# First tiles fed k-outer behind the norm, and forgetting attention as one stream of steps across head borders, in a hybrid transformer layer

## The chip, the cores and the metric

The kernel runs on the 8 cores of one Trainium2 chip. Each core computes one of the eight sequences of the batch, with the same program; the cores exchange nothing. The metric is the device time in microseconds (us) of the slowest core. A trace also gives the span of each core, and where a difference of a few us is at stake this document uses the mean of the eight spans as well, because "the slowest of eight" adds luck to every reading.

Executions of this program come in two states. In the slow one the cores of one die show a lower granted TensorE clock than those of the other, and the time is some per cent longer.

## The reference

One layer: adaLN-modulated RMSNorm, one combined projection, eight heads of forgetting attention (FoX), eight heads of sliding-window attention with rotary embedding and sinks (SWA), output projection, and a squared-ReLU MLP. Sequence and model width are both 2048, head width is 128.

```python
h = rmsnorm(x, g_pre_mix) * (1.0 + sc_a) + sh_a        # sh, sc, gt = parts of silu(c) @ w_mod + b_mod
fq, fk, fv, fg, sq, sk, sv = split(h @ w_in)
log_f = log_sigmoid(fg + b_forget)
fox = forgetting_attention(fq, fk, fv, log_f)          # s[t,u] += cum[t] - cum[u], causal softmax
swa = sliding_window_sink_attention(rope(sq), rope(sk), sv, swa_sinks)
x = x + gt_a * rmsnorm(concat(fox, swa) @ w_out, g_post_mix)
h = rmsnorm(x, g_pre_mlp) * (1.0 + sc_m) + sh_m
x = x + gt_m * rmsnorm(square(relu(h @ w_up)) @ w_down, g_post_mlp)
```

## The kernel before

The program is written as a list of operations in program order; a helper records every operation (`pe` for matmuls, `act` for ScalarE, `cp`, `ts`, `tt`, `stt` for VectorE or GpSimd) and works out the semaphores. So all matmuls of the profile carry one line number, L387, all ScalarE operations L404, VectorE's L407 (two tensors), L412 (scalar and two tensors), L418 and L421 (copy); groups are told apart by the tiles in them.

The names that matter: a *bank* is one of the eight parts of PSUM, the memory into which TensorE writes its products and from which another engine has to read them before the bank is free again. `hT` is the normed input, transposed, in four tiles of 512 tokens and 16 chunks `k`. `R1` is a ring of five 0.5 MB buffers (`ring_67` to `ring_71` in the trace) for the projection's weight stripes, `qh` holds the first two q stripes, `RH` four buffers for the weights of the shift vector (`rsh`), `RM` those of the scale vector. `xstA` and `xstB` hold the input of even and odd tiles. The shift is not added to `hT`: each stripe instead gets a bias column, a product of the stripe with the shift vector `shb`.

The first tile is multiplied *k-outer* (the loop over the chunks is the outer one: each chunk is used by all products in turn, where k-inner finishes one product first) while its chunks are made; tiles 1 to 3 follow with one product after the other:

```python
    def wave0(k):
        h = hT(0, k)
        for i, b in enumerate((qh[0], R1.bufs[W["k"]])):
            pe([mm(banks[PJ[i]](), b(slice(k * 128, k * 128 + 128)), h, k == 0, k == KC - 1)], [b(), h], [banks[PJ[i]]()])
        b = R1.bufs[W["v"][k // 8]]
        kk = k % 8
        for i in range(2):
            ob = banks[OB[i]]
            pe([mm(ob(bi * 256, bi * 256 + 256), hT(0, k, slice((2 * i + bi) * 128, (2 * i + bi) * 128 + 128)),
                   b(slice(kk * 256, kk * 256 + 256)), k == 0 and bi == 0, k == KC - 1 and bi == 1) for bi in range(2)], [b(), h], [ob()])
        fg_mm(0, k, banks[SB[0]])
    # ... weight loads, statistics and norm of tile 0 and of tile 1 around wave0(0..15), cut ...
    F.side = [mods(0, F.pend)]
    for t in range(1, NT):
        jobs = {}
        if t + 1 < NT:
            def at(i, f):
                jobs.setdefault(i, []).append(f)
            for q in range(4):
                at(5 + 3 * q, lambda q=q: n_sq(t + 1, q))
                at(8 + 3 * q, lambda q=q: n_stat(t + 1, q))
            at(18, lambda: n_rstd(t + 1))
            for k in range(KC):
                at(19, lambda k=k: n_z(t + 1, k))
        last = t == NT - 1
        gens = [g_qh(0, t, ev_q(0)(t)), g_fm(sk0, t, ev_k(0)(t), last), g_fg(t)]
        gens += [g_v(sv0, 2 * t + i, vX, last and i == 1) for i in range(2)]
        i = 0
        for g in gens:
            for _ in g:
                for j in jobs.get(i, []):
                    j()
                i += 1
                if last and i % 4 == 0:
                    F._side()
        if t == 1:
            dma("pool", qh[1](), src1(("A", I_Q + 1)), "qh1")
            R1.start(3)
            x_load(3)
```

`g_qh`, `g_fm`, `g_fg` and `g_v` are generators that issue a quarter of a 16-chunk product (four 128x512 matmuls or their equal) and then yield; they take turns on two PSUM banks. The same generators are the *filler* of attention: `F.fill(w)` issues that much projection work between two steps of attention.

The bias columns of the rotary stripes, and a FoX step. A step (`h`, `j`, `kb`) has a score matmul (`qk`), a VectorE subtraction of the decay row and a ScalarE exponential (`expo`), and two products (`pv`). The decay row of head and tile is broadcast from DRAM into one of two buffers `cfb`:

```python
    def sw_bias(i, b):
        bk = fm_col(b, banks[SF[St.sb % 3]])
        act(bs(slice(i, i + 1)), bk(0, 1), AF.Copy)
        act(bsw(slice(i, i + 1), p=(0, 64)), bk(0, 1, p=(64, 128)), AF.Copy)
        act(bsw(slice(i, i + 1), p=(64, 128)), bk(0, 1, p=(0, 64)), AF.Copy)

    def cf_load(h, j):
        i = St.cf % 2
        St.cf += 1
        cf_slot[(h, j)] = cfb[i]
        dma("sp", cfb[i](), dram(T["crow"][h:h + 1, j * TS:j * TS + TS].broadcast_to([128, TS]), "crow", j), f"cf{i}")

    def fox_list(h):
        return [(h, j, kb) for j in range(NT) for kb in range(4 * j + 4)]

    def qk(st):
        h, j, kb = st
        if kb == 0:
            if (h, j) not in cf_slot:
                cf_load(h, j)
            nj = (h, j + 1) if j + 1 < NT else (h + 1, 0)
            if nj[0] < 8 and not (nj[1] == 0):
                cf_load(*nj)
        bk = banks[SF[St.sb % 3]]
        St.sb += 1
        c0 = max(0, kb - 4 * j) * 128
        diag = kb >= 4 * j
        q = qT[h % 2](slice(j * TS + c0, j * TS + TS))
        kk = kT[h % 2](slice(kb * 128, kb * 128 + 128))
        mms = [mm(bk(c0, TS), kk, q, True, not diag)]
        r = [kk, q]
        if diag:
            mms.append(mm(bk(c0, c0 + 128), ident(), maskc(), False, True))
            r += [ident(), maskc()]
        pe(mms, r, [bk()])
        steps[st] = (bk, c0)

    def expo(st):
        h, j, kb = st
        bk, c0 = steps[st]
        tt(bk(c0, TS), bk(c0, TS), cf_slot[(h, j)](slice(c0, TS)), ALU.subtract)
        p = Pb[St.pb % NPB]
        St.pb += 1
        act(p(slice(c0, TS)), bk(c0, TS), AF.Exp, bias=Ctok(slice(kb * 8 + h, kb * 8 + h + 1)))
        steps[st] = (p, c0)

    def pv(st):
        h, j, kb = st
        p, c0 = steps.pop(st)
        nkb = 4 * j + 4
        ob = banks[OB[0]]
        db = banks[DB]
        v = V_OF[h](kb, slice((h % 2) * 128, (h % 2) * 128 + 128))
        pp = p(slice(c0, TS))
        pe([mm(ob(c0, TS), v, pp, kb == 0, kb == nkb - 1), mm(db(c0, TS), ones(), pp, kb == 0, kb == nkb - 1)],
           [v, pp, ones()], [ob(), db()])
        if kb == nkb - 1:
            os = accs[1]
            act(rr(), db(), AF.Ln)
            cp(os(), ob())
            act(rr(), rr(), AF.Exp, scale=-1.0)
            tt(mix(h, slice(j * TS, j * TS + TS)), os(), rr(), ALU.mult)
```

And the heads, one after the other; `fox` starts each head with three steps that have no filler, and ends it by draining the filler:

```python
    def fox(h, prefill, la=LA, skip=0, drain=True):
        L = fox_list(h)
        n = len(L)
        for i in range(la):
            qk(L[i])
            expo(L[i])
        tot = prefill
        for i in range(n):
            if i + la < n:
                qk(L[i + la])
            w = tot / (n - skip) / 2 if i >= skip else 0
            F.fill(w)
            pv(L[i])
            if i + la < n:
                expo(L[i + la])
            F.fill(w)
        if drain:
            F.drain()

    # order of the heads
    F.main = [sk_(0), svpair(), sq_(0), sq_(1), sq_(2), sq_(3)]
    fox(0, 64 * 5 + 128)
    F.main = [sk_(1), sq_(4), sq_(5), sq_(6), sq_(7), q_(2), k_(2)]
    fox(1, 64 * 7)
    F.main = [q_(3), k_(3)]
    swa(0, 128)
    F.main = [vpair(I_V + 6, vX, True)]
    swa(1, 128)
    F.main = [vpair(I_V + 4, vZ, True)]
    fox(2, 128)
    for h in range(3, 7):
        F.main = [q_(h + 1), k_(h + 1)] + ([vbias(h - 3)] if h < 5 else [])
        fox(h, 128)
    # ... later, with the output projection as filler:
    fox(7, 4 * 34, skip=6, drain=False)
```

## Time and profile before

| | before |
|---|---|
| time, median of 3 | 3139.96 us (3139.05 to 3141.51) |
| spans of the eight cores | 3130.6 to 3138.0 us, mean 3135.0 |
| TensorE busy, slowest core | 2910.8 us of 3138.0, 93% |
| from the first MLP matmul to the end | 1823 us, TensorE full up to the tail |

The first view is the page of the slowest core. In the two rows of digits each digit is one fortieth of the span (78 us) in tenths: how busy the engine is, and what clock TensorE was granted. The last line is the chain of work that ended last, by engine.

```profile
span 3138.0 us, 38887 instructions; the slowest of 8 cores (3130.6 to 3138.0 us)
...
PE 2910.8 (93%) x15016; PEld 1379.9 (44%) x15016; DVE 930.5 (30%) x1484; ACT 747.2 (24%) x1229; POOL 469.1 (15%) x614
...
PE   2798988998999899999999999999999999999993
...
PEclk9798988999999899999999999999999999999997
...
PE 82%; DVE 6%; ACT 4%; issue 3%; DMA 3%; POOL 1%; SPq 0%; DVEq 0%; ACTq 0%; POOLq 0%
```

TensorE bounds the kernel, and it is full except in the first 14 digits and in the tail (the last digit), which the change does not touch. In the first 14 the clock row dips with the busy row: an idle TensorE is also a slower one afterwards. Everything that the change can win lies there, before 1100 us.

Next, what TensorE waited for on this core: sum in us, number of waits, longest wait.

```profile
PE bank L387 <- ACT bsw L404: 22.2, 7, 6.8
PE bank L387 <- DVE hT L412: 18.0, 12, 3.6
PE bank L387 <- ACT Pb_102 L404: 14.9, 10, 5.0
```

The first is the bias columns of the rotary stripes, the second the first tiles, the third (with other `Pb` buffers) the steps of FoX, the heads' borders above all.

The timeline of the same core shows one of each. The columns are start, duration, engine, line, operation, output and inputs, shape, count, and in brackets the idle time before and what ended it. First the squares of tile 1's input (101 and 105 us) and the border from tile 1 to tile 2 (146 us), the issue of the first shift weight's load (147 us; on POOL's row, whose queue issues these loads), then a rotary column (475 us), then the border between heads 2 and 3 (790 us), then that between heads 6 and 7 (1032 us).

```profile
101.86 1.91 ACT L404 ACTIVATE sqA_96<-xstB 128x2048 bf16<-128x2048 f32 x1 [1.49 <-DMA xstB<-xP]
105.15 1.91 ACT L404 ACTIVATE sqA_97<-xstB 128x2048 bf16<-128x2048 f32 x1 [1.39 <-DMA xstB<-xP]
...
146.18 1.44 PE L387 MATMUL bank<-hT,qh_204 128*128 128x512 bf16 x4 [3.59 <-DVE hT L412]
...
147.90 0.53 POOL L207 DMA_DIRECT2D rsh_89<-wMB  x1 [91.07 <-DVE hT L412]
...
475.25 0.69 DVE L407 TENSOR_TENSOR skT<-sq_207,acc_208 128x512 bf16<-128x512 f32 x1
...
477.40 0.34 ACT L404 ACTIVATE bsw<-bank 64x1 f32<-64x1 f32 x2
...
477.89 0.48 PE L387 MATMUL bank<-qT_93,kT_94 128*128 128x384 bf16 x1 [6.79 <-ACT bsw L404]
...
792.00 0.69 DVE L407 TENSOR_TENSOR mix<-acc_209,rr 128x512 bf16<-128x512 f32 x1 [0.67 <-ACT rr L404]
792.61 1.49 DVE L407 TENSOR_TENSOR bank<-bank,cfb_80 128x512 f32<-128x512 f32 x3
793.39 0.69 ACT L404 ACTIVATE Pb_102<-bank,Ctok 128x512 bf16<-128x512 f32 x1 [1.50 <-DVE bank L407]
...
794.22 0.22 PE L387 MATMUL bank<-qT_93,kT_94 128*128 128x128 bf16 x1 [3.09 <-ACT Pb_102 L404]
...
1032.80 1.30 DVE L407 TENSOR_TENSOR bank<-bank,cfb_82 128x512 f32<-128x512 f32 x2 [2.14 <-DMA cfb_82<-crow]
...
1034.43 0.58 PE L387 MATMUL bank<-qT_93,kT_94 128*128 128x512 bf16 x1 [1.31 <-ACT Pb_98 L404]
```

At 146 us TensorE has stood 3.59 us until the first chunk of the next tile's `hT` was made. At 477.89 us it has stood 6.79 us: the next score matmul wants a bank that a column still occupies, and ScalarE reads the column only after an exponential that waits for VectorE, which was busy with the rotary embedding. At 794 us it has stood 3.09 us: the old head's last output (792.00) comes first on VectorE, only then are the new head's first scores taken (792.61), and TensorE has no filler to pass the time with. At 1032.80 VectorE has waited 2.14 us for head 7's decay row, and TensorE 1.31. After most waits of this length the matmuls that follow come at half their rate for 3.4 or 6.8 us; the clock is halved.

### The profile page before, as it was taken

The numbers are of one execution on the slowest core, as the hardware profiler recorded it, in microseconds if no ns is written. First come the engines' busy times: TensorE is split into PE (matmuls) and PEld (weight loads), VectorE is DVE, ScalarE is ACT, GpSimd is POOL, SyncE is SP. The second block draws the span as 40 slices with busy tenths as digits, with TensorE's granted clock in tenths as the row PEclk, the third lists the DMA queues.
The fourth block names the chain that finished last, engine by engine and source line by source line (L and its number), as shares of the span: only waits on it lengthen the run. The fifth ranks groups of instructions, "written<-read, shape, count | busy, mean of one in ns | idle before, by whom it ended". The sixth has DMA issues, their size and how long they took to land.

```text
span 3138.0 us, 38887 instructions; the slowest of 8 cores (3130.6 to 3138.0 us)
## 1 busy us (share of the span) xinstructions
PE 2910.8 (93%) x15016; PEld 1379.9 (44%) x15016; DVE 930.5 (30%) x1484; ACT 747.2 (24%) x1229; POOL 469.1 (15%) x614
## 2 busy tenths in 40 slices
PE   2798988998999899999999999999999999999993
PEld 1345533466444344444444444444444444444441
DVE  1323445345555447652111100000233211000005
ACT  1212334364455436432111100000111111000000
POOL 1010100000000155530000011111100000111114
PEclk9798988999999899999999999999999999999997
DMA  9764635433552533354444455455688544444455
GB/s 184 201 104 96 100 69 94 78 61 62 98 97 58 91 121 150 131 127 77 74 79 75 82 100 95 89 99 95 155 188 189 101 80 75 75 80 74 76 101 199
DMA packets 99783, 327.93 MB, mean 105 GB/s; under 512 B 12144, under 2 KB 12272, under 8 KB 93200
## 3 DMA queue, kind: packets, MB, share of 16 engines
q0 software_dynamic: 58896, 213.97, 40.9%
q1 hardware_dynamic: 40704, 111.46, 10.2%
q8 instruction: 122, 2.00, 0.2%
q14 instruction: 61, 0.50, 0.1%
HBM read 497.32 MB, written 42.01 MB: 172 GB/s over the span
## 4 chain that ended last, share of the span: by engine, by line
PE 82%; DVE 6%; ACT 4%; issue 3%; DMA 3%; POOL 1%; SPq 0%; DVEq 0%; ACTq 0%; POOLq 0%
PE bank L387 82%; DVE bank L407 1%; POOL acc_209 L407 1%; DMA xstA<-xP 1%; DVE hT L412 1%; DMA rmod_87<-wMA 1%; ACT acc_208 L404 1%; DVE mixF L412 1%; ACT rr L404 1%; ACT qrot L404 1%; DVE bank L412 1%; DMA xstB<-xP 1%; DMA rsh_89<-wMB 0%; DVE sq_207 L412 0%; DVE acc_208 L412 0%
## 5 line engine op out<-in xcount | busy, mean ns | idle before, releaser
L418 DVE TENSOR_SCALAR bank<-bank 128x512 f32<-128x512 f32 x256 | 166.1, 694 | 638.5 <-PE bank L387 638.5
L421 DVE COPY mixF<-bank 128x512 f32<-128x512 f32 x64 | 41.2, 685 | 842.8 <-PE bank L387 842.8
L387 PE MATMUL bank<-mix,rung_128 128*128 128x512 bf16 x1024 | 226.2, 379 | 0.0
L387 PE MATMUL bank<-mix,rung_129 128*128 128x512 bf16 x1024 | 226.2, 379 | 0.0
L387 PE MATMUL bank<-mix,rung_127 128*128 128x512 bf16 x1024 | 226.2, 379 | 0.0
L387 PE MATMUL bank<-mix,rung_130 128*128 128x512 bf16 x1024 | 226.2, 379 | 0.0
L404 ACT ACTIVATE sq_206<-bank 128x512 f32<-128x512 f32 x30 | 17.9, 597 | 793.0 <-DVE mixF L421 793.0
L387 PEld LDWEIGHTS bank<-mix,rung_129 128*128 128x128 bf16 x1024 | 100.0, 98 | 121.6 <-issue 1.1
L387 PEld LDWEIGHTS bank<-mix,rung_127 128*128 128x128 bf16 x1024 | 100.4, 98 | 120.7
L387 PEld LDWEIGHTS bank<-mix,rung_128 128*128 128x128 bf16 x1024 | 100.4, 98 | 120.7
L387 PEld LDWEIGHTS bank<-mix,rung_130 128*128 128x128 bf16 x1024 | 100.0, 98 | 121.3 <-issue 0.6
L407 DVE TENSOR_TENSOR bank<-bank,cfb_82 128x512 f32<-128x512 f32 x192 | 117.5, 628 | 89.2 <-PE bank L387 86.5
L387 PE MATMUL bank<-hT,ring_69 128*128 128x512 bf16 x512 | 135.5, 396 | 3.2 <-DVE sq_207 L412 2.8
L387 PE MATMUL bank<-hT,ring_68 128*128 128x512 bf16 x384 | 99.5, 391 | 0.0
L407 POOL TENSOR_TENSOR acc_208<-acc_208,sq_206 128x512 f32<-128x512 f32 x62 | 78.5, 1266 | 114.7 <-ACT sq_206 L404 114.7
L387 PE MATMUL bank<-hT,ring_71 128*128 128x512 bf16 x320 | 86.3, 401 | 0.0
L407 POOL TENSOR_TENSOR acc_209<-acc_209,sq_207 128x512 f32<-128x512 f32 x62 | 78.3, 1263 | 44.9 <-ACT sq_207 L404 42.9
L387 PE MATMUL bank<-qT_93,kT_94 128*128 128x512 bf16 (+3 forms) x160 | 57.1, 362 | 30.1 <-ACT bsw L404 11.8
L407 DVE TENSOR_TENSOR bank<-bank,cfb_80 128x512 f32<-128x512 f32 (+3 forms) x128 | 72.8, 594 | 40.6 <-PE bank L387 40.6
L387 PE MATMUL bank<-qT_72,kT_73 128*128 128x512 bf16 (+3 forms) x160 | 56.8, 360 | 25.0 <-ACT bsw L404 10.5
L387 PEld LDWEIGHTS bank<-hT,ring_69 128*128 128x128 bf16 x512 | 50.5, 101 | 60.8 <-issue 13.7
L404 ACT ACTIVATE Pb_98<-bank,Ctok 128x512 bf16<-128x512 f32 (+1 forms) x54 | 35.0, 648 | 86.5 <-DVE bank L407 86.5
(760 smaller groups left out, 4798.1 us busy)
## 6 DMA issues: line engine op xcount, KB each, us to landing
rung_127<-wU POOLq DMA_DIRECT2D x32, 512.0 KB, 6.1
rung_128<-wU POOLq DMA_DIRECT2D x32, 512.0 KB, 6.2
rung_129<-wU POOLq DMA_DIRECT2D x32, 512.0 KB, 6.1
rung_130<-wU POOLq DMA_DIRECT2D x32, 512.0 KB, 6.5
rung_127<-wD POOLq DMA_DIRECT2D x32, 512.0 KB, 6.2
rung_128<-wD POOLq DMA_DIRECT2D x32, 512.0 KB, 6.1
rung_129<-wD POOLq DMA_DIRECT2D x32, 512.0 KB, 6.6
rung_130<-wD POOLq DMA_DIRECT2D x32, 512.0 KB, 6.2
```

The lines of the kernel that those rows point to most:

```text
L387: ins = e.matmul(o, lhsT=l, rhs=rh, start=st, stop=sp)
L404: return P.op("act", lambda e: e.activation(out=out.ap, in_=in_.ap, func=func, **kw), r, [out])
L407: return P.op(eng, lambda e: e.tensor_tensor(out=out.ap, in0=a.ap, in1=b.ap, op=op), [a, b], [out])
L412: return P.op(eng, lambda e: e.scalar_tensor_tensor(out=out.ap, in0=a.ap, scalar=sc, in1=b.ap, op0=op0, op1=op1), r, [out])
L418: return P.op(eng, lambda e: e.tensor_scalar(out=out.ap, in0=a.ap, scalar1=sc, scalar2=None, op0=op), r, [out])
L421: return P.op("dve", lambda e: e.tensor_copy(out=out.ap, in_=a.ap), [a], [out])
```

## The change

Three parts: "FoX heads as one continuous stream of steps across head borders; projections of all four first tiles k-outer behind the norm; shift weights in two free slots". In the diff:

1. **First tiles.** Tiles 1 to 3 also run k-outer (`wave`): each hT chunk is used by q, k, forget gate and v as soon as VectorE has made it. The tiles use two sets of banks. Two of the four shift weights get slots that are free early, and their loads stand in the program before the end of tile 0 instead of after tile 1, and ahead of the loads for head 1.
2. **Forget gate and q bias** get banks of their own after the tiles.
3. **Rotary columns.** VectorE copies the column out of PSUM; ScalarE makes the two swapped halves from that copy, so the bank no longer waits for ScalarE.
4. **Heads as a stream.** Heads 0 and 1, and heads 2 to 7, are each one list of steps. The three steps of lookahead run over the border. The next head's q and k are projected tile by tile in turn (`qk_`), and `begin` issues filler until the tile that a step needs is there. The next head's decay row is loaded ahead.

The core of the diff, with cuts (statistics banks, ring bookkeeping, arguments of `fox` for heads 0 and 1):

```diff
     def sw_bias(i, b):
         bk = fm_col(b, banks[SF[St.sb % 3]])
-        act(bs(slice(i, i + 1)), bk(0, 1), AF.Copy)
-        act(bsw(slice(i, i + 1), p=(0, 64)), bk(0, 1, p=(64, 128)), AF.Copy)
-        act(bsw(slice(i, i + 1), p=(64, 128)), bk(0, 1, p=(0, 64)), AF.Copy)
+        cp(bs(slice(i, i + 1)), bk(0, 1))
+        act(bsw(slice(i, i + 1), p=(0, 64)), bs(slice(i, i + 1), p=(64, 128)), AF.Copy)
+        act(bsw(slice(i, i + 1), p=(64, 128)), bs(slice(i, i + 1), p=(0, 64)), AF.Copy)
 ...
+    def bank_set(t):
+        return [banks[i] for i in ((0, 1, 2, 4, 5), (6, 3, 2, 4, 5))[t % 2]]
+
+    def wave(t, k):
+        ... as wave0, for tile t and bank_set(t), forget gate third ...
+
+    def wave_out(t):
+        b = bank_set(t)
+        act(lf(slice(t * TS, t * TS + TS), p=(0, 8)), b[2](p=(0, 8)), AF.Copy)
+        ... two V banks: the first by ScalarE, the second by VectorE ...
+        ev_q(0)(t)(b[0])
+        ev_k(0)(t)(b[1])
 ...
     n_rstd(1)
     x_load(2)
+    RH.start(0, 2)
+    dma("pool", qh[1](), src1(("A", I_Q + 1)), "qh1")
+    R1.start(3)
 ...
+    for k in range(4):
+        n_z(1, k)
     for t in range(1, NT):
-        ... jobs and gens, one product after the other ...
+        wave_out(t - 1)
+        for k in range(4, KC):
+            n_z(t, k)
+        if t == 1:
+            x_load(3)
+        for k in range(KC):
+            wave(t, k)
+            ... squares and statistics of tile t + 1 at fixed k ...
+        if t + 1 < NT:
+            n_rstd(t + 1)
+            for k in range(4):
+                n_z(t + 1, k)
 ...
-            if nj[0] < 8 and not (nj[1] == 0):
+            if nj[0] < 8 and nj not in ((2, 0),):
                 cf_load(*nj)
 ...
-    def fox(h, prefill, la=LA, skip=0, drain=True):
-        L = fox_list(h)
+    def fox(segs):
+        L = [st for sg in segs for st in fox_list(sg[0])]
         n = len(L)
+        def begin(i):
+            h, j, kb = L[i]
+            if h in done:
+                while done[h] < j:
+                    F._one()
+            qk(L[i])
 ...
+    def qk_(h):
+        s = [R1.acq(("A", I_Q + h)), R1.acq(("A", I_K + h))]
+        done[h] = -1
+        q_bias(h, R1.bufs[s[0]])
+        for t in range(NT):
+            yield from g_fm(s[0], t, ev_q(h)(t), t == NT - 1)
+            yield from g_fm(s[1], t, ev_k(h)(t), t == NT - 1)
+            done[h] = t
 ...
-    fox(2, 128)
-    for h in range(3, 7):
-        F.main = [q_(h + 1), k_(h + 1)] + ([vbias(h - 3)] if h < 5 else [])
-        fox(h, 128)
-    ... and later fox(7, 4 * 34, skip=6, drain=False)
+    fox([(2, lambda: [vpair(I_V + 4, vZ, True)], 128, 0)]
+        + [(h, lambda h=h: [qk_(h + 1)] + ([vbias(h - 3)] if h < 5 else []), 128, 0) for h in range(3, 7)]
+        + [(7, last_head, 4 * 34, 6)])
```

## The prediction

> **What bounds it now.** TensorE: 93% of the 3138 us span on the page, 82% of the chain of waits. From 1320 us to the tail the stretches view shows it 100% busy at full clock; the change touches nothing there. What can be won lies between 110 and 1100 us: in the TensorE timeline about 105 us idle, and about 50 us more lost by running at half clock. The Trainium skill, "TensorE: Matmul & The Clock Gate", Part 1, says that the clock is halved after an idle window of about 3.4 us and returns after a busy one. The trace agrees: after nearly every gap above 2 us, 128x512 matmuls stand 0.43 us apart instead of 0.216, for 3.4 or 6.8 us. So a gap costs about 1.7 us above its length.
>
> **Term 1, first tiles (111 to 205 us).** Before, tiles 1 to 3 wait for the norm: about 3.6 us, then short waits for hT at half clock. The k-outer wave lets TensorE follow VectorE (0.67 us per hT chunk). Two things are paid. A k-outer chunk takes 1.275 us in tile 0 of the trace; k-inner the same matmuls take 1.09: 3 us more per tile. And the next tile's norm still closes after the last chunk: statistics, two ScalarE passes, first hT: 3.2 us idle per border. Neighbouring tiles share banks 2, 4 and 5, and the second V copy stands on VectorE behind four hT chunks: 1.7 us more, then half clock. Estimate: tile 3 ends at 199 instead of 205 us. Gain 6 us (0 to 14).
>
> **Term 2, forget gate and shift columns.** The q bias gets its own banks: 1.5 us. Shift weights come earlier, but their wait is only 1.1 us now.
>
> **Term 3, rotary bias columns.** TensorE waits for ScalarE bsw 22.2 us in 7 waits (waits view). The bank now comes free after one VectorE copy. But that copy stands behind the rotary operations (0.75 + 0.74 + 0.69 us), which wait for ScalarE. In the 6.8 us wait at 471 us it would come about 1 us earlier, in the 3.0 us wait at 540 us no earlier. Gain 4 us.
>
> **Term 4, head borders.** Each head starts with three score matmuls and no filler while VectorE and ScalarE finish the last head. Gaps: 5.0 us at 443, 3.1 at 791, 2.3 at 851, 1.9 at 910, 3.1 at 968, 5.4 at 1027 to 1038: 21 us, and some 10 us of half clock behind them. These go; the 4.8 us at 724, where head 2 begins a stream, stays. Given back: the next decay row is loaded only after the old head's last step and lands after 7 us, while four short steps with filler take 4.6 us; at head 7, without filler, 2 to 3 us stay. Gain 20 us (12 to 28).
>
> **Sum:** 6 + 1.5 + 4 + 20 = 31 us; matmul work is unchanged. Predicted 3109 us, range 3093 to 3125. Faster by over 2%: 0.04; within 2%: 0.95; slower: 0.01.
>
> **Right if** no TensorE gap above 2 us stands at the six borders, about 3 us before tiles 2 and 3, wave chunks take 1.27 us; bsw leaves the waits, VectorE bs appears with 12 us or more; 1320 us onward is only shifted.
>
> **Wrong if** the tile borders are filled after all (term 1 up to 20 us), if the q and k stripes, holding two ring slots, starve the side weights, or if late decay rows stall each border.

## The result, and the profile after

| | before | after |
|---|---|---|
| fast executions | 3138.98, 3139.05, 3139.96, 3141.51 us | 3126.49, 3126.86 us |
| slow executions | none here | 3300.58, 3332.28 us |
| spans of the cores, profiled execution | 3130.6 to 3138.0, mean 3135.0 | 3109.0 to 3124.7, mean 3116.6 |

The ratio of fast executions is 0.9958, with a 95% interval of 0.9934 to 0.9982: the same, by a limit of 2%. Ratios here and below are the mean time of one kernel's fast runs over that of the other's of the same rounds.

So the change is worth 13 us where 31 were expected. The eight cores tell more. This view has the span of each core and its mean granted TensorE clock:

```profile
core 3: 3124.7 us, clock 0.972
...
core 5: 3109.0 us, clock 0.976
```

The span of the best core is by chance the predicted time, the slowest is 15.7 us behind, and the clock goes with the span. Before, best and slowest core were 7.4 us apart. The mean of the eight cores gained 18.4 us.

The page of after, slowest core, with the lines that were shown of before:

```profile
span 3124.7 us, 38905 instructions; the slowest of 8 cores (3109.0 to 3124.7 us)
...
PE 2913.8 (93%) x15016; PEld 1375.2 (44%) x15016; DVE 928.1 (30%) x1489; ACT 748.4 (24%) x1224; POOL 469.1 (15%) x614
...
PE   2799989999999899999999999999999999999993
...
PEclk9899989999999899999999999999999999999996
...
PE 82%; DVE 5%; DMA 4%; ACT 4%; issue 3%; POOL 1%; SPq 0%; DVEq 0%; ACTq 0%; POOLq 0%
```

TensorE's share and busy time are unchanged; three of the first 14 digits of the busy row are one higher. The waits of TensorE on the same core of after, in the same columns as before:

```profile
PE bank L387 <- DVE bs L421: 23.0, 8, 5.0
PE bank L387 <- ACT sqA_97 L404: 17.5, 4, 4.6
...
PE bank L387 <- DVE hT L412: 4.7, 2, 2.4
...
PE bank L387 <- ACT Pb_102 L404: 5.4, 8, 1.1
```

The waits for `hT` fell from 18.0 to 4.7 us and those for `Pb_102` from 14.9 to 5.4. The wait for the rotary column has changed its name, not its size: 22.2 us for ScalarE's copy before, 23.0 for VectorE's copy now. The same places in the timeline of after (core 3): the issue of the two early shift weights (54 us), tile 1's squares and the matmuls behind them (105 to 115 us), the border to tile 2, a rotary column that now stands on the border from head 0 to 1 (440 us), the border of heads 2 and 3 (779 us), and that of heads 6 and 7 (1018 us).

```profile
54.19 0.54 POOL L207 DMA_DIRECT2D rsh_89<-wMB  x1
...
105.25 1.91 ACT L404 ACTIVATE sqA_96<-xstB 128x2048 bf16<-128x2048 f32 x1 [4.51 <-DMA xstB<-xP]
110.88 1.91 ACT L404 ACTIVATE sqA_97<-xstB 128x2048 bf16<-128x2048 f32 x1 [3.71 <-DMA xstB<-xP]
...
112.93 1.87 PE L387 MATMUL bank<-sqA_97,ones 128*128 128x512 bf16 x4 [4.60 <-ACT sqA_97 L404]
114.59 0.63 PE L387 MATMUL bank<-hT,qh_204 128*128 128x512 bf16 x1
...
145.40 0.52 PE L387 MATMUL bank<-hT,qh_204 128*128 128x512 bf16 x1 [2.37 <-DVE hT L412]
...
440.98 0.69 DVE L407 TENSOR_TENSOR mix<-sq_207,acc_208 128x512 bf16<-128x512 f32 x1
441.59 0.15 DVE L421 COPY bs<-bank 128x1 f32<-128x1 f32 x1
...
441.89 0.38 PE L387 MATMUL bank<-qT_93,kT_94 128*128 128x512 bf16 x1 [2.92 <-DVE bs L421]
...
779.47 0.38 PE L387 MATMUL bank<-qT_93,kT_94 128*128 128x512 bf16 x1
...
779.69 0.22 PE L387 MATMUL bank<-maskc,ident 128*128 128x128 bf16 x1
...
1018.00 1.30 DVE L407 TENSOR_TENSOR bank<-bank,cfb_82 128x512 f32<-128x512 f32 x2 [3.31 <-DMA cfb_82<-crow]
...
1019.63 0.59 PE L387 MATMUL bank<-qT_93,kT_94 128*128 128x512 bf16 x1 [3.84 <-ACT Pb_98 L404]
```

What to see: at 779 us the head border is gone, as the prediction said. At 441 us one border gap (4.96 us before) has turned into a wait of 2.92 us for the column's copy, which stands on VectorE right behind the rotary operation of 440.98. At 1018 us the decay row of head 7 comes 3.31 us late and TensorE waits 3.84. And the squares of tile 1's last quarter start at 110.88 us instead of 105.15: the input itself came late, and the whole first stretch with it (on the mean of the eight cores this square starts at 105.0 us before and at 110.4 after). That was in no line of the prediction. The first line of the fence shows what is new there: the two shift weights (the second follows 0.5 us later) are issued at 54 us, not at 147.90. Before, the load waited for VectorE's `hT`, because its buffer overlapped the input of tile 2, from which VectorE was still to make `hT`; in its new slot it waits for nothing and goes 93 us earlier, ahead of tile 1's input (issued at 81 to 83 us in both kernels), although TensorE first uses it at 183 us. The traces show what that does: the loads of this queue, all issued by 57 us, land one after the other, some 6 us apart, the two new ones at 86.5 and 92.5 us and the last (`ring_71`) at 111.4 (core 3; before, on the same core, at 101.8). Until then tile 1's input, whose last quarter lands at 110.7 instead of 105.5, is in flight together with them.

To add this up, I cut the time from the first matmul with `hT` to the first MLP matmul at the same six events in both traces, and split each stretch into idle time of TensorE, loss by half clock (half of the busy time at half clock) and full-clock work. Means of eight cores, each line: length = idle + half clock + work, in us.

| stretch | before | after | gain |
|---|---|---|---|
| first hT matmul to FoX (tiles, head 1's q, k, v) | 208.5 = 35.5 + 17.3 + 155.6 | 200.0 = 26.1 + 10.4 + 163.6 | 8.5 |
| FoX heads 0 and 1 with the rotary filler | 325.7 = 40.1 + 21.7 + 263.9 | 323.5 = 37.4 + 22.2 + 263.8 | 2.2 |
| sliding window | 118.2 = 2.9 + 0.0 + 115.3 | 119.2 = 2.9 + 0.9 + 115.3 | -1.0 |
| FoX heads 2 to 6, up to the first wO matmul | 315.4 = 30.1 + 10.0 + 275.3 | 307.3 = 24.3 + 7.1 + 275.8 | 8.1 |
| rest of head 7, output projection, up to the MLP | 276.1 = 18.1 + 5.4 + 252.6 | 275.3 = 18.7 + 3.9 + 252.8 | 0.8 |
| sum | | | 18.6 |

The 18.6 us hold the whole gain of the mean core (18.4 by the spans); from the MLP on both traces agree. The table also shows the k-outer price: 8 us more of full-clock work in the first row, where 3 us for each of three tiles were predicted. (A few matmul records are missing on two cores of each trace, which moves some 10 us from work to idle there; lengths are not touched.)

A list of TensorE's gaps of 1.5 us and more in FoX heads 0 and 1 says why the second row gave so little. I computed it from the traces, for the slowest core of each, in order of time:

```
before  3.00  3.07  5.34  2.05  3.39  4.96(border)  6.79  1.86  2.97  2.75    sum 36.2, half clock 21.7 (mean of cores)
after   3.00  3.51  2.78  2.48  3.39  2.92(border)  4.98  2.31  3.41  3.19    sum 32.0, half clock 22.2
```

Three gaps got shorter, five got longer by 0.4 us each, and there are ten as before, on each of the eight cores. Half clock comes anew with each such gap, so it did not fall at all.

### The profile page after: what moved, and what is told of

It reads as the page before. It is cut to its first block, busy times and chain, and to the rows that moved or that the text cites. A ratio compares the mean times of both kernels' runs of the same rounds, so it can differ in the third digit from the quotient of the medians.

```text
span 3124.7 us, 38905 instructions; the slowest of 8 cores (3109.0 to 3124.7 us)
## 1 busy us (share of the span) xinstructions
PE 2913.8 (93%) x15016; PEld 1375.2 (44%) x15016; DVE 928.1 (30%) x1489; ACT 748.4 (24%) x1224; POOL 469.1 (15%) x614
## 4 chain that ended last, share of the span: by engine, by line
PE 82%; DVE 5%; DMA 4%; ACT 4%; issue 3%; POOL 1%; SPq 0%; DVEq 0%; ACTq 0%; POOLq 0%
PE bank L387 82%; DVE bank L407 1%; POOL acc_209 L407 1%; DMA xstA<-xP 1%; DMA xstB<-xP 1%; DMA rmod_87<-wMA 1%; ACT acc_208 L404 1%; DVE mixF L412 1%; ACT rr L404 1%; DMA cfb_82<-crow 1%; ACT qrot L404 1%; DMA rsh_90<-wMB 0%; DVE bank L412 0%; DVE sq_207 L412 0%; DVE acc_208 L412 0%
## 5 line engine op out<-in xcount | busy, mean ns | idle before, releaser
L387 PE MATMUL bank<-hT,ring_69 128*128 128x512 bf16 x512 | 139.6, 404 | 3.2 <-DVE sq_207 L412 3.2
L387 PE MATMUL bank<-hT,ring_71 128*128 128x512 bf16 x384 | 101.7, 394 | 0.4 <-DVE kT_73 L421 0.4
L407 POOL TENSOR_TENSOR acc_208<-acc_208,sq_206 128x512 f32<-128x512 f32 x62 | 78.6, 1267 | 113.1 <-ACT sq_206 L404 113.0
L387 PE MATMUL bank<-qT_93,kT_94 128*128 128x512 bf16 (+3 forms) x160 | 57.4, 359 | 24.3 <-DVE bs L421 14.2
L387 PE MATMUL bank<-hT,ring_68 128*128 128x512 bf16 x256 | 67.1, 394 | 1.1 <-DVE kT_73 L421 1.1
L387 PE MATMUL bank<-hT,ring_67 128*128 128x512 bf16 x192 | 58.9, 393 | 0.0
```

Source lines behind the costliest of these rows:

```text
L387: ins = e.matmul(o, lhsT=l, rhs=rh, start=st, stop=sp)
L407: return P.op(eng, lambda e: e.tensor_tensor(out=out.ap, in0=a.ap, in1=b.ap, op=op), [a, b], [out])
```

## The experiments

Twelve kernels were run, all with correct results. The first four shared one chip (the kernel before: fast runs 3143.4 us on average, mean core 3138.3), e5 to e8 a second one (mean core 3138.3 as well), e9 to e12 a third (mean core 3136.2). "Mean core" below is the mean of all cores over all fast executions of a kernel; differences between kernels of different chips are taken through the kernel before. The scatter: single fast executions of one kernel differ by up to 4 us in their mean core, so a difference of 1 us between two kernels is not clear of it.

My theory after the result: the stream does what was expected of it at heads 2 to 6 but less in size; the rotary columns are a wash; and the early shift-weight loads delay the input of tile 1 and eat the gain of the first tiles. Rivals: the k-outer tiles are themselves a loss; or certain cores are always slower, and the cause lies in the chip and not in the kernel.

### e1: the changed kernel again

> The changed kernel once more, as the reference of this chip for the next three. If the spread of its cores (3109 to 3125 us in the first profile) is the luck of where each core's half-clock windows fall, it comes again, but other cores are the slow ones: fast runs 3123 to 3128 us, means of the eight cores 3114 to 3119. If some cores are slow for a fixed reason, cores 0, 3, 4, 6 are the slow ones again.

Fast runs 3129.74, 3132.11, 3131.40 us (three more were slow: 3276.38, 3535.88, 3647.71); ratio 0.9961 (0.9942 to 0.9981); mean core 3123.0, so 15.3 us under the kernel before, and the time itself 12.3 us under it. The slow cores differ from one fast run to the next: core 4 took 3116.3 us in the first and 3111.8 in the second, core 7 took 3112.9 and 3130.3. A fixed set of slow cores is refuted. What stays is that the time lies 8.1 us over the mean core, against 5.0 for the kernel before: 3 us of the shortfall is this. (The values that I had expected were missed by 2 to 4 us, in time and mean; the kernel before is 3 us slower on this chip too.)

### e2: the two early shift weights moved behind tile 1's norm

```diff
     n_rstd(1)
+    gate = [None if dry else P.ops[-1]]
     x_load(2)
-    RH.start(0, 2)
     dma("pool", qh[1](), src1(("A", I_Q + 1)), "qh1")
     R1.start(3)
+    RH.start(0, 2, gate)          # start() passes the extra dependency on to its two loads
```

> The first two shift weights are loaded only after the norm constant of tile 1, instead of while x of tile 1 still comes in. Theory A (these 1 MB share the DMA engines with x of tile 1, whose last square came at 110.9 us instead of 105.2): the last square comes back to about 105 us, tile 1 starts about 5 us earlier, q of head 1 starts at 195 us instead of 200 to 202, and the mean of the cores falls by 4 to 6 us. Theory B (the tiles are late only because a k-outer chunk costs 1.275 us): no change at the start of tile 1, span within 2 us of the changed kernel. Should the shift weights be needed early, a new wait for rsh appears after 180 us.

Fast runs 3123.37, 3119.65, 3122.78 us (one slow: 3385.97), ratio 0.9932 (0.9913 to 0.9952); mean core 3112.9, which is 10.1 us better than e1 on the same chip. In the timeline of core 1 the last square starts at 107.28 us and TensorE stays at full clock:

```profile
107.28 1.91 ACT L404 ACTIVATE sqA<-xstB 128x2048 bf16<-128x2048 f32 x1 [1.32 <-DMA xstB<-xP]
...
109.33 1.02 PE L387 MATMUL bank<-sqA,ones 128*128 128x512 bf16 x4 [1.48 <-ACT sqA L404]
110.19 0.38 PE L387 MATMUL bank<-hT,qh 128*128 128x512 bf16 x1
```

Its two loads are issued at 112 us. The four statistics matmuls take 1.02 us here and 1.87 in after, and the wait before them is 1.48 instead of 4.60. The last square starts at 106.9 us on the mean of the cores, against 113.0 in the traced execution of e1. The stretch up to head 1's q shrank to 127 us, from 132 in after and 133 on the four undisturbed cores of e1, and the two traces (of e1 only the die that was not slow can be used) differ by 5 us in sum. The fast executions that were timed differ by 10; the rest is in no trace that I have, and part of it may be scatter (e2's traced execution is the slowest of its three by mean core, 3114.8 against 3111.9 twice). So 5 us are shown, and up to 10 were measured. The theory holds: two loads of 512 KB that TensorE does not need for another 70 us delayed the one it was waiting for by 5 to 6 us.

### e3: the heads split again

The rest of the change stays, each head is its own list, with a drain between heads and no decay row loaded ahead over the border. Heads 0 and 1 are split in the same way (not shown in the cut).

```diff
-    fox([(2, ...)] + [(h, ...) for h in range(3, 7)] + [(7, last_head, 4 * 34, 6)])
+    for sg in [(2, ...)] + [(h, ...) for h in range(3, 7)] + [(7, last_head, 4 * 34, 6)]:
+        fox([sg])
+        if sg[0] < 7:
+            F.drain()
```

> The changed kernel with every FoX head as a stream of its own again (drained at its end, three score matmuls without filler at the next start); interleaved q and k stripes, tiles and columns stay. My prediction's term 4 says that the stream is worth 20 us: mean of the cores 12 to 28 us above the changed kernel. The decomposition of the two traces says less: heads 2 to 6 lost 5 to 7 us of idle and 3 to 4.5 us of half clock, the border of head 1 only moved into a wait for the rotary column: 7 to 11 us above.

Fast runs 3141.93, 3139.99, 3142.38 us (one slow: 3253.98), ratio 0.9994 (0.9975 to 1.0014); mean core 3132.9, 9.9 us over e1. The stream is worth 10 us, not 20; without it 5 us of the mean core and 2 of the time are left of the change. The border gap is back to the hundredth (timeline, core 1, heads 2 and 3):

```profile
789.46 0.22 PE L387 MATMUL bank<-qT,kT 128*128 128x128 bf16 x1 [3.09 <-ACT Pb L404]
```

FoX 2 to 6 took 317.8 us in this trace, against 307 to 309 in e1, e2 and after. Where the other half went can be read from the gaps of TensorE there, those of 0.4 us and more at the five borders of the kernel before (core 1) and of after (core 3), and for after the new ones of 0.8 us some 25 us behind three of them:

```
border to head   3           4             5             6           7
before           3.09        0.45 + 1.83   0.45 + 1.41   3.09        3.09 + 1.31     sum 14.7
after            -           0.80 + 0.78   1.43 + 0.79   1.06 + 0.81 1.08 + 3.84     sum 10.6
```

The large gap is gone at each border but the last; but small ones stand in its place, and the trace of after names what they wait for: the copy of the v bias column (0.80), the copy of the new head's last k tile (1.06), the old head's normalisation (1.43), late exponentials (0.78 to 1.08), and at head 7 the late decay row (3.84; 2.4 to 3.8 on five of the eight cores; on the other three VectorE does not wait for the row, and TensorE waits 1.61 us a little later). All gaps of 0.5 to 1.5 us in this stretch add up to 7.6 to 9.5 us before and 12.5 to 15.3 after, by core. What the stream surely won is the half clock behind the large gaps (10.0 to 7.1 us).

### e4: the old tile loop in the changed kernel

The code of tiles 1 to 3 and the slots of the shift weights as before; heads, columns and banks of the changed kernel.

> The changed kernel with the first four tiles and the shift weights as before; the stream, the q and k stripes and the columns stay. The traces say that tiles and shift weights gave 4 us up to the start of q of head 1 (136 to 132 us from the first hT matmul), and perhaps 3 us more up to FoX: mean of the cores 4 to 8 us above the changed kernel. My prediction's term 1 said 6 us. If the stream was the whole gain, it is within 2 us of the changed kernel.

Fast runs 3132.45 and 3134.63 us (two slow: 3300.56, 3393.70), ratio 0.9969 (0.9945 to 0.9993); mean core 3121.0, so 2 us *better* than e1. That reads as "the k-outer tiles are worth nothing", and it is not wrong as an account of the whole change. But the stretches differ. Up to FoX, e4 takes 207.0 us and after 200.0 (e1, on its four undisturbed cores: 201.5): in their own place the new tiles win 5.5 to 7 us, which is the predicted 6. It is given back elsewhere: the output projection takes 272.4 us in e4 and 275.3 in after, and FoX 0 and 1 takes 321.0 against 323.5 (322.4 in e1). The first has a visible cause, a wait of 1.79 us in the middle of the output projection that e4 does not have (e8), the second has none that I found. Its ten long gaps are there as in after; what is smaller is the half clock behind them, 19.1 us against 22.2. And e2 says that the early loads, which are part of the same edit, cost more than that. e2 against e4 is the comparison that leaves them out: k-outer tiles with late shift loads against the old tiles, on one chip. The mean core is 8.1 us better (3112.9 against 3121.0), and the stretch up to FoX 11 us shorter (196.0 against 207.0). So the rival, that the k-outer tiles are a loss, is refuted.

### e5: each rotary column early, before the last quarter of the stripe ahead

On top of e2. A column's 16 small matmuls and copies are now issued while the stripe ahead of it still has a quarter of a product to go, so TensorE has something to do while VectorE gets to the copy.

```diff
+    def ropes(items, after=None):
+        for n, (src, i, dst) in enumerate(items):
+            ...
+            for t in range(NT):
+                for q, v in enumerate(g_fm(s, t, ev_rope(i, dst)(t), t == NT - 1)):
+                    if t == NT - 1 and q == 2 and nx:
+                        pre[nx[0]] = R1.acq(("A", nx[0]))
+                        sw_bias(nx[1], R1.bufs[pre[nx[0]]])
+                    yield v
```

> On top of the kernel with the late shift weights: the shift column of the next rotary stripe is computed before the last quarter of the stripe ahead of it, so that the VectorE copy that frees the bank does not stand behind that stripe's last rotary operations. Theory (term 3: the wait is the rotary operations in front of the copy, not the engine that copies): the waits for VectorE bs fall from 23 us in 8 to under 8 us, with 3 to 8 us of half clock, mean of the cores 12 to 22 us below the kernel with the late shift weights. Rival (the wait is the length of the column's matmuls and its latency, wherever it stands): the waits stay near 20 us and so does the time.

Fast runs 3110.03, 3108.09, 3108.60, 3109.86 us (one slow: 3343.71), ratio 0.9891 (0.9876 to 0.9907); mean core 3100.0, which is 12.8 us better than e2 (both through the kernel before), at the lower end of what was expected. From its view of TensorE's waits (us, times, longest):

```profile
PE bank L387 <- DVE bs L421: 10.3, 6, 4.1
```

The wait fell from 23.0 in after to 10.3 us (under 8 was expected), and FoX 0 and 1 from 322.6 to 309.2 us. The idle time there fell only from 37.2 to 31.8; the larger part is half clock, 21.6 to 12.0, because the gaps of 1.5 us and more went from ten to five. So it was never the question which engine copies the column; it was that nothing stood between the column's matmuls and the wait for their bank. This is the largest single gain, on the term that the prediction had put at 4 us.

### e6: unread matmuls at the tile borders

On top of e2: nine 128x512 matmuls into a bank that is about to be overwritten, before tiles 2 and 3, so that TensorE is not idle while the next norm closes.

```diff
+            o = bank_set(t + 1)[0]
+            pe([mm(o(), ones(), sqA[1](i % 4), True, True) for i in range(9)], [ones(), sqA[1]()], [o()])
```

> On top of the kernel with the late shift weights: nine 128x512 matmuls with a result that nobody reads, in the TensorE gap before tiles 2 and 3 where it waits for the norm. Theory (half clock after a gap costs as much as the gap): the gap is 2 us shorter for the trace though the first hT comes no earlier, the first chunks of tiles 2 and 3 run at full clock, and up to q of head 1 the cores lose 2 to 5 us of half clock: mean of the cores 2 to 5 us lower. Rival (half clock comes from the whole stretch, not from the gap; or the added matmuls delay the first chunk): no gain, or 1 to 2 us slower.

Fast runs 3121.39, 3123.94, 3121.77, 3119.53 us (two slow), ratio 0.9932 (0.9914 to 0.9949); mean core 3113.0, the same as e2. At the place itself it works: the wait for hT is 0.43 us instead of 2.37 and the chunks behind it run at full clock (timeline, core 1; the 13 matmuls are four of the statistics and the nine).

```profile
139.63 2.97 PE L387 MATMUL bank<-sqA,ones 128*128 128x512 bf16 x13
143.03 0.38 PE L387 MATMUL bank<-hT,qh 128*128 128x512 bf16 x1 [0.43 <-DVE hT L412]
```

The first stretch shrinks by 3.8 us (126.8 to 123.0: 4.1 less idle, 4.4 less half clock, 4.6 more work). But the whole does not get faster; FoX 2 to 6 is 2.7 us longer in this trace, in part because the decay row at head 7 is late again. Whether the rest is chance I cannot say from one profile; e12 asks again.

### e7: a third buffer for the decay row of head 7

On top of e2: the row of (head 7, tile 1) gets a buffer of its own and is loaded at the end of head 6, so that it need not wait until a buffer comes free.

```diff
+        if (h, j) == (7, 1):
+            cf_slot[(h, j)] = B["cfx"]
+            dma("sp", B["cfx"](), ..., "cfx")
+            return
 ...
+            if (h, j) == (6, 3):
+                cf_load(7, 1)
```

> On top of the kernel with the late shift weights: the decay row of query tile 1 of the last head has a buffer of its own and is loaded while head 6 still runs. Theory (the border to head 7 kept its stall because that row could be loaded only after head 6's last step): the wait of 1.6 to 3.8 us two query steps into head 7 falls under 1 us, and the half clock behind it goes on the cores that had it: mean of the cores 2 to 5 us lower. Rival (the stall is VectorE and ScalarE catching up without filler): the wait stays, now released by the score of VectorE without a DMA in front, and the time is within 1.5 us.

Fast runs 3122.96, 3119.61, 3120.38, 3123.13 us (none slow), ratio 0.9931 (0.9915 to 0.9947); mean core 3112.0, 0.8 us better than e2, where 2 to 5 were expected. The cause of the late start is confirmed: on none of the eight cores does VectorE still wait for a decay row at this border, and in the timeline of core 3 TensorE waits 0.43 us instead of 3.84. On the other seven cores a wait of 1.61 us remains some 4 us later, behind an exponential and with no load in it, as on the undelayed cores of after.

```profile
1014.30 1.29 DVE L407 TENSOR_TENSOR bank<-bank,cfx 128x512 f32<-128x512 f32 x2
...
1015.92 0.38 PE L387 MATMUL bank<-qT,kT 128*128 128x512 bf16 x1 [0.43 <-ACT Pb L404]
```

FoX 2 to 6 goes from 307.4 to 305.3 us. The late row is real but worth at most 1 to 2 us, which is within the scatter.

### e8: the output projection's banks in the other order

On top of e2: the counter that alternates the two projection banks is advanced by one before head 7.

```diff
     acc = next_acc()
+    pj[0] += 1
```

> On top of the kernel with the late shift weights: the two projection banks are used in the other turn from the last head on. Theory (the kernel with the old tiles was 2.7 us faster in the output projection only because an odd number of bank uses lay before it, so that the first tile of the next output group does not meet the bank still being read): the TensorE gap of 1.79 us about 30 us into the output projection's second tile is gone, mean of the cores 1.5 to 4 us lower. Rival (a matter of half-clock windows alone): gap unchanged, time within 1 us.

Fast runs 3121.04 and 3124.15 us (two slow), ratio 0.9934 (0.9913 to 0.9956); mean core 3111.9, 1.0 us better than e2 (1.5 to 4 was expected; this is not clear of the scatter). The last stretch goes from 276.6 to 273.3 us, and the wait of 1.79 us that stands there in the kernel before, in after and in e2 is gone, as it is in e4. So e4 got some 3 us in that stretch by the parity of a counter that the tile loop also advances, and not by its tiles.

### e9: the columns copied by ScalarE, as before

On top of e2, `sw_bias` as in the kernel before.

> On top of the kernel with the late shift weights: the three copies of each rotary shift column are made by ScalarE from PSUM again, as in the kernel before. My prediction's term 3 says that the copy on VectorE gained 4 us: mean of the cores 3 to 5 us higher. The waits of the two traces (22.2 us for bsw before, 23.0 us for bs after, of which 2.9 us came from the head border) say 2 to 3 us of idle and hardly any half clock: 1 to 4 us higher.

Fast runs 3118.10, 3117.51, 3119.84, 3119.20 us (none slow), ratio 0.9931 (0.9913 to 0.9948), where e2 has 0.9932; mean core 26.9 us under the kernel before, e2 25.4. The waits view has the old name and the same sum:

```profile
PE bank L387 <- ACT bsw L404: 22.8, 8, 6.1
```

I had expected e9 to be 1 to 4 us slower. The VectorE copy of the change is worth nothing.

### e10, e11, e12: the parts together

e10 is e2 with e5, e6, e7 and e8. e11 adds an order of the copies at the tile borders: the V copies behind one chunk of hT on VectorE instead of four. (The start of the last two shift weights also moves, from the end of tile 1 to just behind the copies that follow; it is not in the cut.) e12 is e11 without the unread matmuls of e6.

```diff
-    for k in range(4):
-        n_z(1, k)
+    n_z(1, 0)
     for t in range(1, NT):
-        wave_out(t - 1)
-        for k in range(4, KC):
-            n_z(t, k)
+        wave_out(t - 1, 0)            # forget gate and V
+        for k in range(1, 4):
+            n_z(t, k)
+        wave_out(t - 1, 1)            # q and k
+        for k in range(4, KC):
+            n_z(t, k)
```

> Late shift weights, early columns, third decay row, other bank turn and border filling together. If the gains add: e5 stood 13 us below the kernel with the late shift weights, the other three 0 to 1 us each by their times and 2 to 3 us each by their traces, so mean of the cores 3094 to 3099 us, slowest core 3102 to 3108. If half-clock windows give part back elsewhere, the mean stays at 3098 to 3101.

> As e10, and the copies that free the shared V banks stand behind one hT chunk instead of four. Theory (that copy behind four chunks makes the second wait of 1.2 to 1.4 us at each tile border): those waits go, up to q of head 1 about 3 us less: mean 2 to 4 us below e10. Rival (the next hT chunks come later instead, so that TensorE waits for them): within 1 us of e10.

> As e11 without the unread matmuls at the tile borders. If they save 2 to 4 us of half clock there, as the trace of e6 shows up to q of head 1, this one is 2 to 4 us slower on the mean; if what they save is given back later, within 1 us.

| | fast runs, us | ratio to before | mean core, under before |
|---|---|---|---|
| e10 | 3100.27, 3100.47, 3102.61 | 0.9876 (0.9852 to 0.9900) | 42.5 |
| e11 | 3095.66, 3098.93 | 0.9863 (0.9839 to 0.9886) | 48.5 |
| e12 | 3097.07, 3093.70, 3096.36, 3096.43 | 0.9858 (0.9841 to 0.9875) | 47.6 |

The parts add up: e2's 25.4 and the single gains of e5, e6, e7 and e8 over it (12.8, 0, 0.8, 1.0) make 40.0, and e10 measured 42.5. The order of the copies gives 6 us more, of which the traces show 3.4 in the first stretch. The unread matmuls are worth nothing within 1 us: without them, the wait at the tile border is back and the chunks behind it run slowly for 3.4 us (e12, core 1, timeline), but that much work is also saved.

```profile
137.86 0.38 PE L387 MATMUL bank<-hT,qh 128*128 128x512 bf16 x1 [2.37 <-DVE hT L412]
...
141.78 0.63 PE L387 MATMUL bank<-hT,ring 128*128 128x512 bf16 x1
...
143.46 0.38 PE L387 MATMUL bank<-hT,ring 128*128 128x512 bf16 x1
```

e12 is the best version: 1.4% under the kernel before and about 1% under the change as it was made.

## Why the prediction was right or wrong

The class (within 2%) was right, and so was the account of what bounds the kernel: TensorE, with nothing to win after 1320 us. The time was not: 31 us of gain were predicted, 13 measured in time. Fast executions took 3126.5 to 3126.9 us, just outside the range of 3093 to 3125, on its slow side. Three steps failed: "These go" in term 4 (20 us promised, 10 came), "Shift weights come earlier" in term 2, which was given no price (5 to 10 us lost), and "Gain 4 us" in term 3 (nothing came).

| term of the sum | predicted | measured |
|---|---|---|
| 1, first tiles | 6 us | 5.5 to 7 in their own stretch, nothing for the whole (e4); 8 for the whole without the early loads (e2 against e4) |
| 2, forget gate and shift columns | 1.5 us | not measured alone, e4 and before differ by 1.5 up to FoX; early shift loads -5 to -10 (e2) |
| 3, rotary columns | 4 us | 0 (e9) |
| 4, head borders | 20 us | 10 (e3) |
| not in the sum: more spread between cores | - | -3 (e1) |

Of the tests that the prediction set itself, these came out: about 3 us before tile 2 (2.37 and 0.58), chunks of 1.275 us (+8 us of work in the stretch), from 1320 us on only a shift. Half right: four of the six borders have no gap over 2 us, but those to heads 1 and 7 have 2.92 and, on five of eight cores, 2.4 to 3.8; VectorE's `bs` appears in the waits, but with 23.0 us where "12 us or more" stood for what is left after a gain. Of the three dangers named, only the late decay row came, at one border; the one that cost most, a load that overtakes another, was not named.

**Term 4, the step that failed most.** "Gaps: ... 21 us, and some 10 us of half clock behind them. These go", less what was given back, "Gain 20 us". The mechanism was right: the gaps of 3.09 us at heads 3 and 6 are gone and the head's start is filled. The size was wrong twice. First, a gap that is filled on TensorE does not vanish from the chain: the same VectorE and ScalarE work is still to be done around the border (the last output's normalisation, the last k tile, the v bias), and TensorE now meets it in waits of 0.8 to 1.4 us, 6.8 us in all; with the late row's 3.84, 10.6 us stand where 14.7 stood. Second, the border of heads 0 and 1 was counted as cleared, but a rotary column stands right on it and holds a score bank: 2.92 us of 4.96 stay, and with them the half clock. The part about the decay row was right in place ("at head 7, without filler, 2 to 3 us stay"; 2.4 to 3.8 measured on five of the eight cores), and it is worth 0.8 us, which is within the scatter (e7).

**Term 3.** "The bank now comes free after one VectorE copy. But that copy stands behind the rotary operations" was the right description, and the conclusion "Gain 4 us" did not follow from it. Two column waits got shorter (6.79 to 4.98, 5.34 to 2.78 in the cores listed), four grew by 0.4 us, the column at the border is new, and the number of gaps stayed ten. The Trainium skill, "Perfetto Trace Analysis", Tensor Engine Instruction, says that VectorE, ScalarE and GpSimd take their work strictly in order. The traces agree: the copy of 0.15 us at 441.59 comes right after the rotary sum of 440.98, although TensorE had finished the column and stopped 2.9 us before. Moving a copy from one busy queue to another helps only if the new queue reaches it sooner; e5 shows that the order of issue is what counts.

**Term 1.** The k-outer chunk of 1.275 us and the wait at the tile border came as predicted (2.37 us and 0.58 us at tile 2, "about 3 us"), and so did the gain in the stretch, but that the 5.5 to 7 us there match the 6 is luck: without the early loads the new tiles win 11 us in it (e2 against e4), and the loads take some 5 of them back. Missing was the price of "shift weights come earlier", which stands under term 2 as if it could only help: "their wait is only 1.1 us now". In their new slots the two loads wait for nothing, so they go out at 54 us, and tile 1's input, whose last square starts 5.7 us later, pays for it. Taking them away from there was worth 5 us by the traces and 10 by the mean core of the fast executions (e2). In the timeline before the change `xstB` was already what those squares waited for (1.49 and 1.39 us); that was the line to be asked what a further load ahead of it would do.

**Half clock.** The prediction reckoned with 1.7 us a gap. In FoX heads 0 and 1 it is 2.2 us for each gap of 1.5 us and more (22.2 us for ten; in e5 12.0 for five). More important, it goes by the number of gaps and hardly by their length: in the kernel before (core 1) the gap of 5.34 us was followed by 3.41 us of half clock and that of 2.97 us by 6.83. So shortening three gaps saved none of it, and removing five saved 10 us. The prediction quoted an idle window of 3.4 us as agreeing with the trace, beside gaps above 2 us that already halved the clock; the last section has the counts.

**The slowest core.** The prediction took the time of one core as that of the chip. On the mean core the gain was 18.4 us (15.3 on the second chip). After the change the cores lose between 36.6 and 52.5 us to half clock, with the same program, and the span follows: 3109.2 us for 36.6, 3124.7 for 52.5. Before it was 48.7 to 58.8. The Trainium skill, "TensorE: Matmul & The Clock Gate", Part 1, says that the activity window runs freely, so that the same kernel meets it at different phases from run to run; that fits cores which change places between runs (e1). That gaps close to the limit make this a lottery, in which the time is that of the worst of eight, fits these numbers; no run tried it.

**What stays open.** Why the fast executions of e2 gain 5 us that its trace does not show; why the same ten gaps of FoX 0 and 1 cost 3 us less half clock in e4. In the traces of e10 to e12, all fast executions, two cores of one die each lose 34 to 38 us to the clock in FoX 0 and 1. This is not half clock: the granted clock there is 0.81 for some 155 us, and 128x512 matmuls stand 0.263 us apart instead of 0.216. Why it came to that, no run here tried. Their stretch took 311.5 to 314.7 us, against 307.8 to 311.3 on the other cores, because TensorE waited some 15 us less: there a slower TensorE cost 3 us or so, since part of the time it waits for others. The share of term 2 was not tried alone.

## What to carry to other kernels

Count the gaps of TensorE that are long enough to halve the clock, not only their sum: removing one is worth more than shortening several, and a small dependent product (a bias column) should be issued ahead of work that needs nothing from it. Before a load's wait is taken away, ask when it will then be issued, which loads it will overtake, and whether the bounding engine waits for those. When a stall at a border is filled, expect the work of the other engines at that border to come back as several smaller waits, and take half of the gap as the gain, as it came out here, until an experiment says more.

## What the Trainium skill lacked or had wrong

- "TensorE: Matmul & The Clock Gate", Part 1 ("HAM oscillation") and its section "Why this matters for your kernels" ask for no TensorE gaps over about 3 us, or 3.4. Here shorter gaps suffice. I took every gap of 0.5 us and more that began at full clock, between 300 and 1100 us, in the traces of before, after, e2, e5 and e12, eight cores each, and asked whether half clock followed before the next gap: 4% of 873 gaps of 0.5 to 1.0 us, 18% of 257 of 1.0 to 1.5, 68% of 112 of 1.5 to 2.0, 66% of 83 of 2.0 to 2.5, 91% of 53 of 2.5 to 3.0, and 255 of 258 over 3.0 us. (Each gap is counted alone; what its neighbours add to it was not separated.) The stretches at half clock last 3.41 or 6.83 us, 17 of 523 of them longer.
- The same page, Part 1, puts the ramp's penalty at under 1% of a typical span. That speaks of the warm-up and is no bound for a clock that is halved again and again: in this kernel half clock cost 54 us of 3135 before (1.7%), between the first hT matmul and the MLP, and after the change it differed by up to 16 us between cores of one execution.
- No page gives the price of a k-outer order with mixed shapes: 128x512, 128x256 and eight-column matmuls in turn took 1.275 us a chunk, the same matmuls k-inner 1.09 us.
- No page gives a figure that I found for what loads already in flight on the GpSimd-issued queue cost a later load of another queue; here two more loads of 512 KB, issued at 54 us, moved the start of the work on an input issued at 81 to 83 us by 5.4 us (mean of eight cores).
